# Modulation vectors for later layers: sums down the partitions and a turn through TensorE, or one multiply-and-sum along the row

## The chip, the cores and the metric

The kernel runs on one core of one Trainium2 chip. Its time is the device time of one execution in microseconds (us), the median over several runs. All five engines of the core take part: TensorE (PE; its weight loads are shown as PEld), VectorE (DVE), ScalarE (ACT), GpSimd (POOL) and SyncE (SP), which only issues DMAs.

## The reference

One step of a two-layer network on 128 prompt tokens and 512 latent tokens, model width 2048, all in float32. Each layer has a modulation (adaLN) with a shift, a scale and a gate for each of the two token groups:

```python
def adaln(cvec, w, b):
    mod = jax.nn.silu(cvec) @ w + b          # w: (2048, 3 * 2048)
    return jnp.split(mod, 3, axis=-1)
...
    for l in range(DEPTH):
        sh_p, sc_p, g_p = adaln(c_ctx[None, :], w_ada[l], b_ada[l])
        sh_s, sc_s, g_s = adaln(c, w_ada[l], b_ada[l])
        hp = rmsnorm(xp, norm_pre[l]) * (1.0 + sc_p[:, None]) + sh_p[:, None]
        hs = rmsnorm(xs, norm_pre[l]) * (1.0 + sc_s[:, None]) + sh_s[:, None]
        ...                                  # mixer of the layer: op, os_
        xp = xp + g_p[:, None] * rmsnorm(op, norm_post[l])
        xs = xs + g_s[:, None] * rmsnorm(os_, norm_post[l])
```

Layer 0's mixer has windowed attention (8 heads, "A") and neighbourhood attention (8 heads, "B") side by side; layer 1's is a retention. Both have an input and an output projection, which hold nearly all of the arithmetic.

## The kernel before

Activations lie transposed: features on the 128 partitions (16 tiles of 128), 640 tokens along the row. The projections run in float32 precision out of rounded parts: every weight tile of 128x512 (`wraw`) is split into a rounded part `whi` (ACT, L291) and the rest `wlo` (DVE, L292), every activation into `hi` and `lo`, and PE multiplies hi by whi, lo by whi and hi by wlo (L1370, L1311).

The program is one hand-ordered stream. Its main loop goes over slots; a slot is one split weight tile and 24 to 30 matmuls on it. `ahead(s)` splits the tile of slot s+4 and loads that of slot s+7. Four split tiles fit in SBUF, so a split waits until PE has finished the slot four before. Ahead of each slot `step_all()` moves four lanes one step on, in this order: `chain` (norms after a projection), `rope` (rotation of A's queries and keys), `heads` (attention blocks: scores on PE, softmax on DVE and ACT, transposes, values) and `adal` (the later modulation). A lane takes one new item each step, and the later stages of an item come at the steps after it. Every engine works through its own queue in program order.

The modulation of layer 0's shift and scale is needed at once and is made by PE at the start. The **later modulation**, layer 0's gate and layer 1's shift, scale and gate (8192 outputs for each of two vectors), is spread by the lane `adal` over the slots of layer 0's input projection, which runs from 150 to 990 us. There the weights have their *input* features on the partitions, as 256 tiles of 128x512 (`adaraw`, L787). For each tile and each of the two vectors, DVE multiplies the tile by the vector's value of its partition and adds it to an accumulator `adaacc` of 128x512 (L804). For one tile in five or so, the second vector's share goes another way: ACT scales the tile in place (L801), and POOL adds it (L802). After 16 tiles, a quarter's sums still lie spread over the 128 partitions. They are split into three bfloat16 parts (`adab`, L812, L814, L818), and PE adds them up over the partitions, 128 columns at a time, each as weights against a column of ones:

```python
    def ada_cols(ids, dst, q4):
        if ids[0] == 0:
            parts3["ps"] = dense()
        ps = parts3["ps"][:, 8 * (ids[0] > 0):]
        for c in range(4):
            for v in range(2):
                for i in ids:
                    mm(ps[:, 2 * c + v:2 * c + v + 1], lhsT=parts3[i, v][:, 128 * c:128 * c + 128], rhs=ones16,
                       start=(i == ids[0]), stop=(i == ids[-1]))
```

It is called twice for each of the 16 quarters, first for one part (8 matmuls), then for two (16). DVE copies and adds the results into `gg`, `sh` and `am` (L832, L834), and `ada_fin` adds the bias and makes scale and gate ready. `dense()` is one of five PSUM banks that the projections use in turn.

The prediction also speaks of two places in layer 0's attention. A query of an A head is rotated by `rope_item`: swapped quarters by DMA into `rp`, products on DVE (L574) and POOL (L575), and their sum on DVE (L578). One step after the sum is issued, PE's first score of the head (L722) follows. In a block's softmax DVE adds the bias and takes the maximum in one instruction (L688, `tensor_tensor_reduce`), ACT takes the exponential (L698), DVE normalizes (L705), and PE transposes (L742).

Of the kernel before, what the change touches and what calls it, by code (L numbers as in the profile page):

```python
# [11 lines left out]
F32 = mybir.dt.float32  # L12
F32R = mybir.dt.float32r
BF16 = mybir.dt.bfloat16
AF = mybir.ActivationFunctionType
ALU = mybir.AluOpType
# [3 lines left out]
KT = 16  # L20
# [5 lines left out]
EPS = 1e-6  # L26
SCALE = 128 ** -0.5
NEG = -1e30
ADA_UNITS = (2, 1, 2, 2, 2, 1, 2, 2, 2)
PLACE = {("w_in_even", "W"): 2, ("w_in_even", "X"): 1, ("w_out_even", "W"): 1, ("w_in_odd", "W"): 2,  # L30
         ("w_in_odd", "X"): 1, ("w_out_odd", "W"): 0}
GAPS = (2, 1)
# [130 lines left out]
def body(tc, io):  # L163
    nc = tc.nc
    top = ExitStack()
    top.enter_context(tc.manual_schedule())
    main = top.enter_context(tc.tile_pool(name="main", bufs=1))
# [4 lines left out]
    lo = main.tile([128, KT, T], F32R, name="lo")  # L172
    y = main.tile([128, KT, T], F32, name="y")
    ident = main.tile([128, 128], F32, name="ident")
    ones = main.tile([128, 128], F32, name="ones")
    ones16 = main.tile([128, 1], BF16, name="ones16")
    cols = main.tile([128, 2, 5, KT], F32, name="cols")
    gn = main.tile([128, KT], F32, name="gn")
    sink = main.tile([128, 8], F32, name="sink")
    cvec = main.tile([128, KT, 2], F32, name="cvec")  # L180
    mhalf = main.tile([128, 1], F32, name="mhalf")
    sh = [main.tile([128, KT, 2], F32, name=f"sh{l}") for l in range(2)]
    am = [main.tile([128, KT, 2], F32, name=f"am{l}") for l in range(2)]
    gg = [main.tile([128, KT, 2], F32, name=f"gg{l}") for l in range(2)]

    def bg(tag):
        return psb.tile([128, 512], F32, name="ps_" + tag, tag=tag)

    def dense():
        return psd.tile([128, 512], F32, name="ps_d", tag="d")  # L190

    mm = nc.tensor.matmul
# [3 lines left out]
    nc.sync.dma_start(cvec, io["cT"])  # L196
    nc.sync.dma_start(cols, io["cols"])
    nc.sync.dma_start(ident, io["ident"])
    nc.vector.memset(ones, 1.0)
    nc.vector.memset(mhalf, -0.5)  # L200
    nc.vector.memset(ones16, 1.0)

    def rstd_cols(acc, nt, pool, out, alloc=None):

        ps = alloc() if alloc else bg("T")
        accs = acc if isinstance(acc, list) else [acc]
        for t in range(nt):
            for i, ac in enumerate(accs):
                mm(ps[:, t:t + 1], lhsT=ac[:, 128 * t:128 * t + 128], rhs=ones[:, :1],
                   start=(i == 0), stop=(i == len(accs) - 1))  # L210
        v = pool.tile([128, 5], F32, name="msq")
        nc.vector.tensor_scalar(v[:, :nt], ps[:, :nt], 1.0 / D, EPS, op0=ALU.mult, op1=ALU.add)
        nc.gpsimd.tensor_tensor(out[:, :nt], v[:, :nt], mhalf.to_broadcast([128, nt]), op=ALU.pow)
# [8 lines left out]
    def rstd_bc(dg, nt, out, alloc=None):  # L222
        for b0 in range(0, nt, 4):
            n = min(4, nt - b0)
            ps = alloc() if alloc else bg("S")
            for t in range(n):
                mm(ps[:, 128 * t:128 * t + 128], lhsT=ones, rhs=dg[:, b0 + t, :], start=True, stop=True)
            nc.scalar.activation(out[:, 128 * b0:128 * (b0 + n)], ps[:, :128 * n], AF.Copy)
        return ps

# [39 lines left out]
    for job, (w, kind, role, col, gs) in enumerate(STREAM):  # L270
        u0 = FIRST_UNIT[BLOCK_AT[w, kind, col]]
        n = UNITS[kind]
# [23 lines left out]
    with ExitStack() as st:  # L296
        s1 = st.enter_context(tc.tile_pool(name="s1", bufs=1))
        sraw = st.enter_context(tc.tile_pool(name="sraw", bufs=SRAW))
        x = y
# [66 lines left out]
        def norm_a():  # L366
            rstd_cols(acc[0], 5, s1, rcol, dense)
# [129 lines left out]
    adal = Lane(done)  # L497
# [27 lines left out]
    at = L0.enter_context(tc.tile_pool(name="at", bufs=1))  # L525
# [252 lines left out]
            block(j)  # L778


    ada_raw = {}
    NADA = 16 * KT

    def ada_load(i):
        if i < NADA:
            ada_raw[i] = at.tile([128, 512], F32, name="adaraw", bufs=4)
            nc.sync.dma_start(ada_raw[i], io["ada1"][i])  # L787

    accs = {}

    def ada_unit(i, pool=False):
        kt = i % KT
        r = ada_raw.pop(i)
        if kt == 0:
            for v in range(2):
                accs[v] = at.tile([128, 512], F32, name="adaacc", bufs=2)
                nc.vector.tensor_scalar(accs[v], r, cvec[:, kt, v:v + 1], None, op0=ALU.mult)
        else:
            for v in range(2):
                if v == 1 and pool:  # L800
                    nc.scalar.activation(r, r, AF.Copy, scale=cvec[:, kt, 1:2])  # L801
                    nc.gpsimd.tensor_tensor(accs[1], accs[1], r, op=ALU.add)  # L802
                else:
                    nc.vector.scalar_tensor_tensor(accs[v], r, cvec[:, kt, v:v + 1], accs[v], op0=ALU.mult, op1=ALU.add)  # L804
    parts3 = {}

    def ada_part(i):

        for v in range(2):
            parts3[i, v] = at.tile([128, 512], BF16, name="adab", bufs=4)  # L810
            if i < 2:
                nc.scalar.activation(parts3[i, v], accs[v], AF.Copy)  # L812
            else:
                nc.vector.tensor_tensor(parts3[i, v], accs[v], parts3[1, v], op=ALU.subtract)  # L814

    def ada_less():
        for v in range(2):
            nc.vector.tensor_tensor(accs[v], accs[v], parts3[0, v], op=ALU.subtract)  # L818

    def ada_cols(ids, dst, q4):  # L820

        if ids[0] == 0:
            parts3["ps"] = dense()
        ps = parts3["ps"][:, 8 * (ids[0] > 0):]
        for c in range(4):
            for v in range(2):
                for i in ids:
                    mm(ps[:, 2 * c + v:2 * c + v + 1], lhsT=parts3[i, v][:, 128 * c:128 * c + 128], rhs=ones16,
                       start=(i == ids[0]), stop=(i == ids[-1]))
        d = dst[:, 4 * q4:4 * q4 + 4, :].rearrange("p c v -> p (c v)")  # L830
        if ids[0] == 0:
            nc.vector.tensor_copy(d, ps[:, :8])  # L832
        else:
            nc.vector.tensor_tensor(d, d, ps[:, :8], op=ALU.add)  # L834

    def ada_fin(l, what, dst):
        for v in range(2):
            d = dst[:, :, v]
            nc.vector.tensor_tensor(d, d, cols[:, l, 2 + what, :], op=ALU.add)
            if what == 1:  # L840
                nc.vector.scalar_tensor_tensor(d, d, 1.0, cols[:, l, 0, :], op0=ALU.add, op1=ALU.mult)
            if what == 2:
                nc.vector.tensor_tensor(d, d, cols[:, l, 1, :], op=ALU.mult)

    ada_items = []
    for q, (l, what) in enumerate(((0, 2), (1, 0), (1, 1), (1, 2))):
        dst = {0: sh, 1: am, 2: gg}[what][l]
        for q4 in range(4):
            i0 = KT * (4 * q + q4)
            for n in ADA_UNITS:  # L850
                ada_items.append([[lambda i=i0 + j, p=(j == 1 and i0 % KT < 12): ada_unit(i, p) for j in range(n)],
                                  [lambda i=i0 + 4 + j: ada_load(i) for j in range(n)]])
                i0 += n
            ada_items.append([[lambda: ada_part(0), ada_less]])
            ada_items.append([[lambda: ada_part(1)]])
            ada_items.append([[lambda d=dst, q=q4: ada_cols((0,), d, q), lambda: ada_part(2)], [lambda d=dst, q=q4: ada_cols((1, 2), d, q)]
                              + ([lambda l=l, w=what, d=dst: ada_fin(l, w, d)] if q4 == 3 else [])])
    i = 0
    while i < len(ada_items):
        it = ada_items[i]  # L860
        if len(it) == 2 and i % (len(ADA_UNITS) + 3) == len(ADA_UNITS) + 2 and i + 1 < len(ada_items):
            it = [x + z for x, z in zip(it, ada_items[i + 1])]
            i += 1
        i += 1
        adal.add([lambda st=st: [f() for f in st] for st in it])
    for i in range(4):
        ada_load(i)


# [45 lines left out]
    def queue_chain(l, gi):  # L915
# [11 lines left out]
        def n1(acc):  # L927
            def f():
                st["rc"] = cp.tile([128, 5], F32, name="rcol", bufs=2)
                rstd_cols(c[acc, gi], nt, cp, st["rc"])  # L930
                st["dg"] = rstd_diag(st["rc"], nt, cp)
            return f
# [397 lines left out]
    s = 0  # L1330
    while s < NS:
        job, kind, role, gs, unit, half, i, ni, w = slots[s]
# [13 lines left out]
        i0 = KP // 4 if role[0] == "rest" else 0  # L1346
# [94 lines left out]
def prepare(inp):  # L1441
    f = np.float32
    a = {k: np.asarray(v) for k, v in inp.items()}
    m = constants()
# [26 lines left out]
    wada = a["w_ada"]  # L1471
    w0 = wada[0].reshape(4, 4, 128, 3, 16, 128)
    ada0 = w0[:, :, :, 0:2].transpose(4, 0, 2, 1, 3, 5)
    m["ada0"] = np.ascontiguousarray(ada0.reshape(64, 128, 1024))
    w1 = wada.reshape(2, 16, 128, 12, 512)
    pieces = [(0, i) for i in range(8, 12)] + [(1, i) for i in range(12)]
    m["ada1"] = np.ascontiguousarray(np.stack([w1[l, :, :, p, :] for l, p in pieces], 0).reshape(256, 128, 512))
    W = {n: a[n][0] for n in ("w_in_even", "w_out_even", "w_in_odd", "w_out_odd")}
    wg = W["w_in_even"][:, 4608:]
    m["wfirst"] = np.ascontiguousarray(np.stack(  # L1480
# [32 lines left out]
```

## Time and profile before

| | |
|---|---|
| time, median of 3 runs | 2534.35 us (2533.91 to 2534.43) |
| the profiled execution's own time | 2534.7 us |
| its span in the trace | 2532.9 us |
| busy in the span: PE, DVE, ACT, POOL | 97%, 59%, 40%, 15% |
| matmuls | 17808 |
| mean granted clock of PE | 0.995 |
| HBM traffic | 325.51 MB read, 15.99 MB written |

The trace is of the profiled execution, whose span is 1.8 us shorter than its own time. Busy time of an engine is that in which at least one of its instructions runs; instructions of one engine overlap a little at their ends, so that a group's count times its mean can be above its busy time. "Idle before" is the engine's idle time just before an instruction, put down to what released it.

### The profile page before, as it was taken

How to read it: one execution, taken by the hardware profiler on the slowest of the kernel's cores; microseconds unless marked ns; L12 is line 12 of the kernel's file. 1: busy time of each engine (PE TensorE's matmuls, PEld its weight loads, DVE VectorE, ACT ScalarE, POOL GpSimd, SP SyncE). 2: the span in 40 equal slices, each digit the busy share in tenths (PEclk: the TensorE clock that was granted, in tenths of full speed). 3: DMA queues.
4: the chain of work that ended last, by engine and by line, in shares of the span. 5: the costliest groups of instructions: out<-in, count | busy, mean ns of one | idle time of the engine just before them, and what ended most of it. 6: DMA issues, size and time to landing. Idle time of an engine off the chain costs nothing.

```text
span 2532.9 us, 45640 instructions
## 1 busy us (share of the span) xinstructions
PE 2459.2 (97%) x17808; PEld 2383.1 (94%) x17808; DVE 1499.3 (59%) x2834; ACT 1006.8 (40%) x2140; POOL 389.6 (15%) x445
## 2 busy tenths in 40 slices
PE   5999999999999999999999999999999999999997
PEld 3699898999999999998999999999999999999996
DVE  6578787787777875338853535353525355363364
ACT  3233454443343335445653333233323333344443
POOL 1012221112112110114200101010101011011132
PEclk9999999999999999999999999999999999999998
DMA  9855444445545532436543121212121221215374
GB/s 373 319 171 178 148 138 145 127 136 183 174 155 172 174 132 86 160 131 224 188 159 128 63 80 63 88 59 86 61 88 59 80 80 63 80 59 179 124 238 130
DMA packets 186441, 347.12 MB, mean 137 GB/s; under 512 B 20912, under 2 KB 45872, under 8 KB 185712
## 3 DMA queue, kind: packets, MB, share of 16 engines
q1 hardware_dynamic: 182368, 333.25, 39.7%
q0 software_dynamic: 3712, 10.82, 1.2%
q8 instruction: 139, 2.28, 0.4%
q14 instruction: 78, 0.64, 0.1%
q10 hardware_dynamic: 144, 0.13, 0.0%
HBM read 325.51 MB, written 15.99 MB: 135 GB/s over the span
## 4 chain that ended last, share of the span: by engine, by line
PE 69%; DVE 4%; issue 2%; ACT 1%; DMA 1%; POOL 0%; SPq 0%; DVEq 0%; ACTq 0%; POOLq 0%
PE ps_d L1370 49%; PE ps_d L1311 12%; PE ps_O L1250 2%; DVE wlo L292 1%; DVE adaacc L804 1%; PE ps_O L1154 1%; PE ps_S L1154 1%; PE ps_O L753 1%; PE ps_T L1228 1%; ACT whi L291 1%; PE ps_S L1242 1%; DMA wraw<-i_wpack 0%; PE ps_T L742 0%; DVE y L974 0%; PE ps_T L1141 0%
## 5 line engine op out<-in xcount | busy, mean ns | idle before, releaser
L1370 PE MATMUL ps_d<-hi,whi 128*128 128x384 f32 (+1 forms) x3808 | 999.0, 316 | 0.7 <-ACT whi L291 0.6
L1370 PE MATMUL ps_d<-hi,wlo 128*128 128x384 f32 (+1 forms) x3808 | 977.1, 310 | 7.4 <-DVE wlo L292 7.0
L1370 PE MATMUL ps_d<-lo,whi 128*128 128x384 f32 (+1 forms) x3808 | 972.6, 309 | 0.0
L292 DVE TENSOR_TENSOR wlo<-wraw,whi 128x512 fp32r<-128x512 f32 x732 | 565.2, 775 | 595.8 <-ACT whi L291 591.0
L1370 PEld LDWEIGHTS ps_d<-hi,whi 128*128 128x128 f32 x3808 | 632.8, 189 | 11.7 <-issue 4.3
L1370 PEld LDWEIGHTS ps_d<-hi,wlo 128*128 128x128 f32 x3808 | 628.9, 189 | 13.0 <-DVE wlo L292 12.2
L1370 PEld LDWEIGHTS ps_d<-lo,whi 128*128 128x128 f32 x3808 | 628.2, 188 | 0.0
L291 ACT ACTIVATE whi<-wraw 128x512 fp32r<-128x512 f32 x732 | 454.8, 626 | 432.9 <-PE ps_d L1370 220.6
L804 DVE SCALAR_TENSOR_TENSOR adaacc<-adaraw,cvec,adaacc 128x512 f32<-128x512 f32 x400 | 276.8, 743 | 5.8 <-POOL adaacc L802 5.7
L802 POOL TENSOR_TENSOR adaacc<-adaacc,adaraw 128x512 f32<-128x512 f32 x80 | 103.0, 1288 | 714.0 <-ACT adaraw L801 711.2
L1311 PE MATMUL ps_d<-whi,hi 128*128 128x256 f32 x960 | 150.9, 287 | 0.8 <-ACT qT L654 0.8
L1311 PE MATMUL ps_d<-whi,lo 128*128 128x256 f32 x960 | 144.3, 280 | 0.0
L1311 PE MATMUL ps_d<-wlo,hi 128*128 128x256 f32 x960 | 144.3, 280 | 0.0
L801 ACT ACTIVATE adaraw<-adaraw,cvec 128x512 f32<-128x512 f32 x80 | 57.9, 724 | 207.7 <-DVE adaacc L804 149.3
L1311 PEld LDWEIGHTS ps_d<-whi,hi 128*128 128x128 f32 x960 | 128.0, 188 | 4.9 <-issue 1.4
L1311 PEld LDWEIGHTS ps_d<-wlo,hi 128*128 128x128 f32 x960 | 126.5, 188 | 0.0
L1311 PEld LDWEIGHTS ps_d<-whi,lo 128*128 128x128 f32 x960 | 126.5, 188 | 0.0
L890 POOL TENSOR_TENSOR acc<-acc,sq 128x384 f32<-128x384 f32 (+1 forms) x56 | 56.1, 1002 | 425.9 <-ACT sq L886 425.6
L698 ACT ACTIVATE p<-p,small 128x384 f32<-128x384 f32 (+1 forms) x64 | 42.9, 671 | 148.3 <-DVE small L690 148.3
L1146 DVE SCALAR_TENSOR_TENSOR fr<-ps_T,kdec,fr 128x256 fp32r<-128x256 f32 x64 | 31.0, 484 | 95.8 <-ACT fr L1145 95.8
L1235 ACT ACTIVATE sS<-sT 128x128 fp32r<-128x128 f32 x40 | 12.4, 311 | 147.9 <-DVE sT L1234 147.9
L1262 POOL TENSOR_TENSOR mv<-mv,mhalf 128x1 f32<-128x1 f32 x40 | 22.1, 552 | 299.5 <-DVE mv L1261 299.5
(248 smaller groups left out, 2427.8 us busy)
## 6 DMA issues: line engine op xcount, KB each, us to landing
wraw<-i_wpack SPq DMA_DIRECT2D x732, 256.0 KB, 2.8
adaraw<-i_ada SPq DMA_DIRECT2D x256, 256.0 KB, 2.7
sraw<-i_ada SPq DMA_DIRECT2D x64, 512.0 KB, 6.3
y<-i_xTp SPq DMA_DIRECT2D x4, 1280.0 KB, 8.6
wf<-i_wfirst SPq DMA_DIRECT2D x20, 256.0 KB, 5.9
bias<-i_biasB POOLq DMA_DIRECT2D x8, 640.0 KB, 4.9
x_scratch<-y SPq DMA_DIRECT2D x8, 384.0 KB, 3.8
xres<-x_scratch SPq DMA_DIRECT2D x8, 384.0 KB, 6.9
```

The lines of the kernel that those rows point to most:

```text
L291: nc.scalar.activation(h, r, AF.Copy)
L292: nc.vector.tensor_tensor(l, r, h.bitcast(F32), op=ALU.subtract)
L698: nc.scalar.activation(p[:, :nk], src, AF.Exp, bias=sm[:, 0:1], accum_out=sm[:, 1:2])
L801: nc.scalar.activation(r, r, AF.Copy, scale=cvec[:, kt, 1:2])
L802: nc.gpsimd.tensor_tensor(accs[1], accs[1], r, op=ALU.add)
L804: nc.vector.scalar_tensor_tensor(accs[v], r, cvec[:, kt, v:v + 1], accs[v], op0=ALU.mult, op1=ALU.add)
L890: nc.gpsimd.tensor_tensor(c["acc", gi], c["acc", gi], sq[:, :w], op=ALU.add)
L1146: nc.vector.scalar_tensor_tensor(t[:, 1, :], ps[:, :256], R["kdec"][:, d, h:h + 1], t[:, 0, :].bitcast(F32), op0=ALU.mult, op1=ALU.subtract)
L1154: mm(ps[:, 256 * d:256 * d + 256], lhsT=k[:, kp, 128 * d:128 * d + 128], rhs=v[:, vp, ch, :], start=(i == 0), stop=(i == 2))
L1250: mm(ab, lhsT=t["q"][:, qp, d, :], rhs=t["S"][d][sp].rearrange("p i e -> p (i e)"), start=(d == 0 and i == 0), stop=(d == 1 and i == 2))
L1311: mm(pss[j][:, o:o + 256], lhsT=xp[:, k, c0:c0 + 128], rhs=wp[:, 256 * kk:256 * kk + 256], start=(i == 0 and kk == 0 and p == 0 and t in ( ...
L1370: mm(pss[gi][:, :b - a], lhsT=wp[:, 128 * kk:128 * kk + 128], rhs=xp[:, k, a:b], start=(k == 4 * i0 and p == 0), stop=(k == KT - 1 and p = ...
```

## The change

The weights of the later modulation are laid out with the *output* features on the partitions and the input features along the row: 64 groups of 128 outputs, each in two halves of 1024 inputs, 128 tiles of 128x1024. The two vectors lie along the row as well, the same on all partitions (`adacb`, 1024 inputs of both at a time, 1 MB), and ACT applies SiLU to them there. For a tile and a vector DVE does one `tensor_tensor_reduce`: product with the vector, summed along the row into one column of `gg`, `sh` or `am`; the second half starts from the first half's sum. ACT, POOL and PE do nothing for it any more, apart from SiLU. The 128 units (one tile, both vectors) are spread over 172 steps of the lane. Half-way the other half of the vectors is loaded, with five empty steps behind it. Tiles have two buffers of 4 KB a partition where they had four of 2 KB.

```diff
-ADA_UNITS = (2, 1, 2, 2, 2, 1, 2, 2, 2)
+ADA_SLOTS = 172
+ADA_REST = 5
...
-                mm(ps[:, 128 * t:128 * t + 128], lhsT=ones, rhs=dg[:, b0 + t, :], start=True, stop=True)
+                mm(ps[:, 128 * t:128 * t + 128], lhsT=one.to_broadcast([128, 128]), rhs=dg[:, b0 + t, :], start=True, stop=True)
...
-    NADA = 16 * KT
+    ada_dst = [(gg[0], 0, 2), (sh[1], 1, 0), (am[1], 1, 1), (gg[1], 1, 2)]
+    NADA = 2 * 4 * KT
+    cb = at.tile([128, 2, 1024], F32, name="adacb")
...
-            ada_raw[i] = at.tile([128, 512], F32, name="adaraw", bufs=4)
+            ada_raw[i] = at.tile([128, 1024], F32, name="adaraw", bufs=2)
             nc.sync.dma_start(ada_raw[i], io["ada1"][i])
...
-    def ada_unit(i, pool=False):
-        kt = i % KT
+    def cb_load(half):
+        nc.sync.dma_start(cb, io["cb"][half])
+
+    def cb_silu(v):
+        nc.scalar.activation(cb[:, v, :], cb[:, v, :], AF.Silu)
+
+    def ada_unit(i):
+        half, f = divmod(i, 4 * KT)
+        q, n = divmod(f, KT)
+        dst, l, what = ada_dst[q]
         r = ada_raw.pop(i)
-        if kt == 0:
-            for v in range(2):
-                accs[v] = at.tile([128, 512], F32, name="adaacc", bufs=2)
-                nc.vector.tensor_scalar(accs[v], r, cvec[:, kt, v:v + 1], None, op0=ALU.mult)
-        else:
-            for v in range(2):
-                if v == 1 and pool:
-                    nc.scalar.activation(r, r, AF.Copy, scale=cvec[:, kt, 1:2])
-                    nc.gpsimd.tensor_tensor(accs[1], accs[1], r, op=ALU.add)
-                else:
-                    nc.vector.scalar_tensor_tensor(accs[v], r, cvec[:, kt, v:v + 1], accs[v], op0=ALU.mult, op1=ALU.add)
...
         for v in range(2):
...
+            out = r if v else at.tile([128, 1024], F32, name="adajunk")
+            d = dst[:, n, v:v + 1]
+            nc.vector.tensor_tensor_reduce(out=out, in0=r, in1=cb[:, v, :], scale=1.0, scalar=d if half else 0.0,
+                                           op0=ALU.mult, op1=ALU.add, accum_out=d)
+        if half and n == KT - 1:
+            ada_fin(l, what, dst)
...
+    at_unit = 0
+    for s in range(ADA_SLOTS):
+        if at_unit * ADA_SLOTS <= s * NADA:
+            if at_unit == NADA // 2:
+                adal.add([lambda: cb_load(1), None, lambda: cb_silu(0), lambda: cb_silu(1)])
+                for _ in range(ADA_REST):
+                    adal.add([None])
+            adal.add([lambda i=at_unit: ada_unit(i), lambda i=at_unit: ada_load(i + 2)])
+            at_unit += 1
+        else:
+            adal.add([None])
+    cb_load(0)
+    for v in range(2):
+        cb_silu(v)
+    for i in range(2):
         ada_load(i)
```

The functions `ada_part`, `ada_less` and `ada_cols` go, and the old list of items with them.

The first place is DVE's queue from the rotated query of the first A head to the head's first softmax. Before, one step's share of the modulation is up to four instructions of 512 columns between the rope's product (L574) and its sum (L578):

```order
L574 TENSOR_TENSOR qT<-rp,cosT 128x512
L804 SCALAR_TENSOR_TENSOR adaacc<-adaraw,cvec,adaacc 128x512 x4
L292 TENSOR_TENSOR wlo<-wraw,whi 128x512
L578 TENSOR_TENSOR qT<-qT,rp 128x512
L804 SCALAR_TENSOR_TENSOR adaacc<-adaraw,cvec,adaacc 128x512 x4
```

Of the change, at the same head (line numbers are lower by one here; `ISA` on two tiles is the multiply-and-sum, the `ISA` of 128x1 behind it reads its sum out):

```order
L573 TENSOR_TENSOR qT<-rp,cosT 128x512
L805 ISA adajunk,sh_77<-adaraw,adacb 128x1024
L805 ISA sh_77 128x1
L805 ISA adaraw,sh_77<-adaraw,adacb 128x1024
L805 ISA sh_77 128x1
L291 TENSOR_TENSOR wlo<-wraw,whi 128x512
L577 TENSOR_TENSOR qT<-qT,rp 128x512
```

The four instructions of 512 columns have become one unit of two instructions of 1024; the split and the rope's sum stay behind it.

The second place is ACT's queue during the last A head, where the change reloads the vectors. Before:

```order
L698 ACTIVATE p,small<-p,small 128x384
L700 ACTIVATE small<-sink,small 128x1
L801 ACTIVATE adaraw<-adaraw,cvec 128x512
L744 ACTIVATE pt<-ps_T 128x512
L698 ACTIVATE p,small<-ps_S,small 128x128
L700 ACTIVATE small<-sink,small 128x1
L291 ACTIVATE whi<-wraw 128x512
L744 ACTIVATE pt<-ps_T 128x384
```

Of the change:

```order
L697 ACTIVATE p,small<-p,small 128x384
L699 ACTIVATE small<-sink,small 128x1
L795 ACT_TABLE_LOAD
L795 ACTIVATE adacb<-adacb 128x1024
L743 ACTIVATE pt<-ps_T 128x512
L697 ACT_TABLE_LOAD
L697 ACTIVATE p,small<-ps_S,small 128x128
L699 ACTIVATE small<-sink,small 128x1
L795 ACT_TABLE_LOAD
L795 ACTIVATE adacb<-adacb 128x1024
L290 ACTIVATE whi<-wraw 128x512
L743 ACTIVATE pt<-ps_T 128x384
```

The scaling of a tile is gone from ACT, and two SiLU instructions with three table loads stand between two exponentials; the program has 31 table loads in all where it had 27.

## Rows read from the trace of the kernel before

**Rows 1.** The page's first part: busy us, share of the span, instructions.

```profile
PE 2459.2 (97%) x17808; PEld 2383.1 (94%) x17808; DVE 1499.3 (59%) x2834; ACT 1006.8 (40%) x2140; POOL 389.6 (15%) x445
```

**Rows 2.** All engines' busy us in the stage 150 to 990, then clock, DMA.

```profile
150.00:990.00 840.00, 821.86 (x6087) 799.17 (x6086) 650.24 (x1254) 353.20 (x761) 161.92 (x174) 0.99 0.48 153
```

**Rows 3.** Waits of PE, 150 to 1000 us: total us, times, longest.

```profile
PE ps_S L722 <- DVE qT L578: 11.0, 5, 4.3
PE ps_T L742 <- DVE p L705: 3.8, 5, 1.7
PE ps_S L725 <- DVE small L688: 1.6, 1, 1.6
```

**Rows 4.** Two windows of 40 us: engines' busy us, PEclk, DMA share.

```profile
270.00:310.00 40.00, 39.21 (x278) 37.58 (x276) 29.94 (x66) 18.38 (x41) 8.58 (x9) 0.96 0.40 126
390.00:430.00 40.00, 35.72 (x250) 34.47 (x249) 30.86 (x61) 18.56 (x43) 10.12 (x10) 0.91 0.38 119
```

**Rows 5.** Timeline of weight loads (PEld): start us, duration us, line, count.

```profile
192.15 0.36 PEld L828 LDWEIGHTS <-adab 128*128 128x128 bf16 x8
192.44 0.30 PEld L1370 LDWEIGHTS ps_d<-hi,whi 128*128 128x128 f32 x2
...
195.68 0.30 PEld L1370 LDWEIGHTS ps_d<-hi,wlo 128*128 128x128 f32 x2
196.09 0.47 PEld L828 LDWEIGHTS <-adab 128*128 128x128 bf16 x16
196.48 0.30 PEld L1370 LDWEIGHTS ps_d<-hi,whi 128*128 128x128 f32 x2
```

**Rows 6.** DVE groups by form, 150 to 990: busy us, mean ns, idle before.

```profile
L804 DVE SCALAR_TENSOR_TENSOR adaacc<-adaraw,cvec,adaacc 128x512 f32<-128x512 f32 x400 | 276.8, 743 | 5.8 <-POOL adaacc L802 5.7
L292 DVE TENSOR_TENSOR wlo<-wraw,whi 128x512 fp32r<-128x512 f32 x189 | 179.2, 950 | 143.7 <-ACT whi L291 143.4
L688 DVE CUSTOM_DVE_ANT_0 p<-ps_S,bias,sink 128x512 f32<-128x512 f32 x16 | 11.9, 744 | 0.0
L688 DVE CUSTOM_DVE_ANT_0 p<-ps_S,bias 128x512 f32<-128x512 f32 x16 | 10.9, 684 | 2.7 <-PE ps_S L725 1.6 <-PE ps_S L728 1.1
L688 DVE CUSTOM_DVE_ANT_0 p<-ps_S,bias 128x384 f32<-128x384 f32 x16 | 8.8, 550 | 5.3 <-PE ps_S L725 3.6 <-PE ps_S L728 1.7
L688 DVE DVE_READ_ACCUMULATOR2_ANT small<- 128x1 f32 x64 | 5.2, 81 | 0.0
```

**Rows 7.** Busy us of instructions on tile adaacc, 150 to 990.

```profile
150.00:990.00 840.00, 329.40 (x496) 37.54 (x64) 103.03 (x80) 0.99 0.48 153
```

**Rows 8.** Waits of the whole span, ACT's on DVE: us, times, longest.

```profile
ACT adaraw L801 <- DVE adaacc L804: 149.3, 54, 5.7
```

**Rows 9.** Timeline of DVE around the first query head, 262 to 269 us.

```profile
262.11 1.37 DVE L292 TENSOR_TENSOR wlo<-wraw,whi 128x512 fp32r<-128x512 f32 x1 [1.31 <-ACT whi L291]
263.40 0.94 DVE L595 TENSOR_TENSOR y<-y,ps_d 128x128 f32<-128x128 f32 x3
264.26 0.93 DVE L574 TENSOR_TENSOR qT<-rp,cosT 128x512 f32<-128x512 f32 x1
...
267.76 0.68 DVE L292 TENSOR_TENSOR wlo<-wraw,whi 128x512 fp32r<-128x512 f32 x1
268.37 0.68 DVE L578 TENSOR_TENSOR qT<-qT,rp 128x512 f32<-128x512 f32 x1
```

**Rows 10.** Timeline of PE at the same place; brackets: idle time and releaser.

```profile
269.10 0.70 PE L722 MATMUL ps_S<-kT,qT 128*128 128x256 f32 x2 [3.66 <-DVE qT L578]
```

**Rows 11.** DMA issues: KB each, median us from issue to landing.

```profile
sraw<-i_ada SPq DMA_DIRECT2D x64, 512.0 KB, 6.3
bias<-i_biasB POOLq DMA_DIRECT2D x8, 640.0 KB, 4.9
```

**Rows 12.** Timeline of ACT around a table load; the ACTIVATE is a SiLU.

```profile
335.89 1.28 ACT L520 ACT_TABLE_LOAD   x1
337.19 0.83 ACT L520 ACTIVATE y<-ps_d 128x128 f32<-128x128 f32 x3
```

More of the change, by code (lines that the diff above doesn't have):

```diff
@@ L174, in body @@
     ident = main.tile([128, 128], F32, name="ident")
-    ones = main.tile([128, 128], F32, name="ones")
-    ones16 = main.tile([128, 1], BF16, name="ones16")
+    one = main.tile([128, 1], F32, name="one")
     cols = main.tile([128, 2, 5, KT], F32, name="cols")
@@ L198, in body @@
     nc.sync.dma_start(ident, io["ident"])
-    nc.vector.memset(ones, 1.0)
+    nc.vector.memset(one, 1.0)
     nc.vector.memset(mhalf, -0.5)
-    nc.vector.memset(ones16, 1.0)
     def rstd_cols(acc, nt, pool, out, alloc=None):
@@ L208, in rstd_cols @@
             for i, ac in enumerate(accs):
-                mm(ps[:, t:t + 1], lhsT=ac[:, 128 * t:128 * t + 128], rhs=ones[:, :1],
+                mm(ps[:, t:t + 1], lhsT=ac[:, 128 * t:128 * t + 128], rhs=one,
                    start=(i == 0), stop=(i == len(accs) - 1))
@@ L781, in body @@
     ada_raw = {}
-    NADA = 16 * KT
+    ada_dst = [(gg[0], 0, 2), (sh[1], 1, 0), (am[1], 1, 1), (gg[1], 1, 2)]
+    NADA = 2 * 4 * KT
+    cb = at.tile([128, 2, 1024], F32, name="adacb")
     def ada_load(i):
         if i < NADA:
-            ada_raw[i] = at.tile([128, 512], F32, name="adaraw", bufs=4)
+            ada_raw[i] = at.tile([128, 1024], F32, name="adaraw", bufs=2)
             nc.sync.dma_start(ada_raw[i], io["ada1"][i])
-    accs = {}
-    def ada_unit(i, pool=False):
-        kt = i % KT
-        r = ada_raw.pop(i)
-        if kt == 0:
-            for v in range(2):
-                accs[v] = at.tile([128, 512], F32, name="adaacc", bufs=2)
-                nc.vector.tensor_scalar(accs[v], r, cvec[:, kt, v:v + 1], None, op0=ALU.mult)
-        else:
-            for v in range(2):
-                if v == 1 and pool:
-                    nc.scalar.activation(r, r, AF.Copy, scale=cvec[:, kt, 1:2])
-                    nc.gpsimd.tensor_tensor(accs[1], accs[1], r, op=ALU.add)
-                else:
-                    nc.vector.scalar_tensor_tensor(accs[v], r, cvec[:, kt, v:v + 1], accs[v], op0=ALU.mult, op1=ALU.add)
@@ L805, in body @@
-    parts3 = {}
-    def ada_part(i):
-        for v in range(2):
[L810 to L834, printed above, removed]
+    def cb_load(half):
+        nc.sync.dma_start(cb, io["cb"][half])
@@ L843, in ada_fin @@
                 nc.vector.tensor_tensor(d, d, cols[:, l, 1, :], op=ALU.mult)
[L845 to L866, printed above, removed]
+    at_unit = 0
[13 more added lines that the diff above has]
+    for i in range(2):
         ada_load(i)
@@ L1474, in prepare @@
     m["ada0"] = np.ascontiguousarray(ada0.reshape(64, 128, 1024))
-    w1 = wada.reshape(2, 16, 128, 12, 512)
-    pieces = [(0, i) for i in range(8, 12)] + [(1, i) for i in range(12)]
-    m["ada1"] = np.ascontiguousarray(np.stack([w1[l, :, :, p, :] for l, p in pieces], 0).reshape(256, 128, 512))
+    w1 = np.concatenate([wada[0][:, 4096:], wada[1]], 1).T.reshape(4 * KT, 128, 2, 1024)
+    m["ada1"] = np.ascontiguousarray(w1.transpose(2, 0, 1, 3).reshape(8 * KT, 128, 1024))
+    cc = np.stack([a["c_ctx"].reshape(2, 1024), a["c"][0].reshape(2, 1024)], 1)
+    m["cb"] = np.ascontiguousarray(np.broadcast_to(cc[:, None], (2, 128, 2, 1024)))
     W = {n: a[n][0] for n in ("w_in_even", "w_out_even", "w_in_odd", "w_out_odd")}
```

## The prediction

> **What bounds the kernel now.** I read the page's first part first: PE is busy for 97% of the span [rows 1]. The edit touches one stage, layer 0's input projection, so the next view is the windows of that stage. From 150 to 990 us PE is busy for 821.86 of 840 us, DVE for 650.24 (77%), ACT for 353.20 and POOL for 161.92 [rows 2]. PE is the bound there, and DVE has a quarter of its time free. A change therefore pays only by what it takes out of PE's queue, or out of the waits in which PE stands still; microseconds saved on ACT or POOL count for nothing by themselves.
>
> [...] The waits of PE in the stage: 11.0 us for the rotated queries, 3.8 us for normalized probabilities, 1.6 us for a maximum [rows 3], all three late DVE work. [...] And the weight loads' timeline, for what the 24 column matmuls of a quarter really take of PE's time.
>
> Why is DVE late with a quarter of its time free? The waits of ACT answer: it stood for 149.3 us, 54 times, with its scaling of a tile, since DVE had not yet read that tile for the other vector [rows 8]. Behind the scaling in ACT's queue is the next split `whi`, and DVE's `wlo` waits for that: the row at 262.11 shows 1.31 us of it. The engines wait for each other in a ring. And that `wlo`, beside POOL's addition, takes 1.37 us, where the next one, at 267.76, takes 0.68 [rows 9]; over the stage its mean is 950 ns [rows 6].
>
> **The change part by part.**
>
> *PE's columns go.* In the timeline the 8 loads of the first call start at 192.15 and the next slot's at 192.44: 0.29 us. The second call is seen against the pace: the two loads ahead of it start at 195.68 and take 0.30, so the next slot would have begun at 195.97 and begins at 196.48: 0.51 us, a short wait for `adab` in it [rows 5]. 0.80 us for a quarter, 16 quarters: **12.8 us**. Over all sixteen I allow 11.5 (without the wait) to 15.
>
> *DVE's work changes form.* The instructions on `adaacc`, the splits into bfloat16 included, took 329.40 us [rows 7]. The new one has a close relative in the trace, the softmax's `tensor_tensor_reduce`: 550 ns for 384 columns and 684 for 512 with a constant as start, 1.05 ns a column, so 684 + 512 x 1.05 = 1220 ns for 1024; 744 for 512 with a start from SBUF, so 1280; and 81 ns to read the sum [rows 6]. One of its operands is in PSUM; the nearest row with both in SBUF is L804, 743 ns for 512 [rows 6], which gives the same 1280. A unit is two of them, about 2.65 us, and 128 units 339 us: 10 more than before. Against that `wlo` loses POOL's company: (0.95 - 0.69) x 189 = 49 us. DVE falls to some 611 us, 73%. Nothing of that is on the path as long as DVE is ahead of PE.
>
> *The ring is cut.* ACT no longer touches the tiles, so `whi` follows PE at once. I walk DVE's queue at the first A query, by the rows of the order: product, unit, `wlo`, sum. With three additions before the product the step is 0.94 + 0.93 + 2.65 + 0.68 + 0.68 = 5.9 us by the rows for these instructions [rows 9], and the sum is due two steps after the step's start, 7 us at a slot of 12 x 0.29 = 3.5 us (the pace of the two loads at 195.68 [rows 5]). It comes in time, where before it ended at 269.05 and PE had stood for 3.66 us [rows 9, 10]. At the later heads the order of the change often has no unit at all between product and sum. Of the 11.0 us I keep 1 and take **10.0**. Of the other 5.4 I take half, **2.7**: these are softmax steps, in which the work itself fills most of a slot. For both the bounds are nothing, as new waits might take their place, and all of it.
>
> *The clock.* 0.04 x 40 + 0.09 x 40 = 5.2 us of work lost at the lower level [rows 4]. [...]
>
> *The reload half-way.* SP's queue has the 1 MB load behind unit 63's tile loads; weights are seven slots ahead there, so no tile is late for it. ACT gets two SiLUs and four table loads more. A table load takes 1.28 us, and the SiLUs behind it start 0.02 us after its end; three of them, 640 columns in all, take 0.83 us [rows 12], so 1024 columns at most 1.33. Together 7.8 us of ACT, which is 42% busy over the stage [rows 2], in two steps of about 4.4 us (840 us for 189 splits [rows 2, 6]). ACT is late there by 3 us at most, while the transposed probabilities it copies are due one step on. I charge **2 us**, between 0 and 5, as the load may land late too: 640 KB take 4.9 us [rows 11], so 1 MB at most twice that by estimate, against two steps.
>
> [...]
>
> *Hidden at no cost.* The first 1 MB and its two SiLUs stand in ACT's queue ahead of the split for slot 4, which PE needs four slots, 14 us, after the first; by the same estimate the load takes under 9.8 us and the SiLUs under 2.7. Tiles: the load for unit i+2 waits for unit i to end, and the unit comes two steps later at the earliest. That leaves 2 x 4.4 - 2.65 = 6.2 us, or 4.4 us where no head runs, for 512 KB. By rows that takes from under 4.9 (640 KB, alone) to 6.3 us (512 KB in a full queue) [rows 11]. So DVE may stand up to 2 us now and then; `wlo` has three slots of lead, and one step in four has no unit. The column of ones read with stride 0 serves a few matmuls. The lane takes 178 steps where it took 177 items, so nothing is left over for the end of the stage.
>
> Sum: 12.8 + 10.0 + 2.7 + 4.2 - 2 = 27.7 us. The profiled execution's own 2534.7 is 0.35 above the median, its span lies 1.8 below. 2534.7 - 27.7 = 2507.0, less 0.35 for the median: **2507 us**.
>
> **The rivals.** 0.2% (5 us) is about what a measurement of this kernel can tell from no change.
>
> *Only the columns count.* DVE stays at three quarters, now in blocks of 2.65 us that nothing can pass, and tiles with two buffers; the softmax's waits grow as the rope's shrink. For it: rows 3 are all DVE's lateness, and a step with a unit and a softmax holds about 5 us against a slot of 4.4. Against it: the ring is gone. Then 2534.35 - 12.8 + 2 = 2523.5.
>
> *The gain is eaten.* As before, but 80 attention blocks lose 0.15 us more each behind a block: another 12 us, 2535, no change.
>
> *DVE becomes the bound, slower.* If the new instruction takes two beats a column with both operands in SBUF, it is 0.15 + 1024 x 2.1 ns = 2.3 us, a unit 4.8. DVE's other work is (650.24 - 329.40 - 49) / 189 = 1.44 us a slot, and there are 128/189 = 0.68 units a slot: 4.7 us against PE's (840 - 28)/189 = 4.3. Then 189 x 0.4 = 75 us come on top of 2507: 2582. It decides from a unit of 4.2 us on. L804's 743 ns for two operands in SBUF [rows 6] speak against it.
>
> **How the numbers follow.** Forecast, with its own range of 2498 (15 + 11.0 + 5.4 + 5.2 - 0 saved) to 2518: 0.58. Only the columns, 2518 to 2527: 0.24. Eaten, 2528 to 2540: 0.09. DVE-bound: 0.09. The predicted time is the first one's. 2498 to 2527 holds the first two, 0.82. Faster by over 0.2% is below 2529.3: 0.82; within 0.2%: 0.08; slower: 0.10.
>
> **What would show it.** Right: no matmul of one column in the stage, 384 fewer in all; the new instruction at 1.2 to 1.3 us; `wlo` in the stage near 700 ns; PE's wait for the rotated query below 2 us in all; clock 1.00 in the windows of the stage; the end of the stage some 28 us earlier and everything behind it unchanged. Wrong: PE waiting for `p` or `wlo` by more than 6 us in the stage, DVE waiting for `adaraw` by more than 2 us at a time, or the new instruction above 2 us.

## The result: 39.6 us faster, 3 us beyond the range

The changed kernel takes 2494.77 us (median of 4 runs, 2493.65 to 2495.88), the kernel before 2534.39 beside it: a ratio of 0.9843, with a 95% interval of 0.9831 to 0.9854. The forecast was 2507 and the range ended at 2498. The gain comes out of the one stage, and the rest of the kernel is as before to within 1.4 us. This row is the first use of the gate of layer 0, just behind the stage, in ACT's timeline of the changed kernel (start us, duration us):

```profile
958.43 0.73 ACT L859 ACTIVATE y<-ps_d,gg 128x128 f32<-128x128 f32 x2
```

and this the same instruction in ACT's timeline of the kernel before:

```profile
998.07 0.73 ACT L892 ACTIVATE y<-ps_d,gg 128x128 f32<-128x128 f32 x2
```

It comes 39.6 us earlier, as much as the medians differ by; over their whole spans the two traces differ by 41.0. The page's first part of the changed kernel, to be held against [rows 1], has 384 matmuls fewer and less work on DVE, ACT and POOL:

```profile
PE 2437.9 (98%) x17424; PEld 2368.5 (95%) x17424; DVE 1444.4 (58%) x2817; ACT 936.4 (38%) x2004; POOL 287.6 (12%) x365
```

The windows of the changed kernel's stage, with the columns of [rows 2], and two pieces of 40 us with the times of those in [rows 4]:

```profile
150.00:960.00 810.00, 810.00 (x5756) 794.09 (x5755) 600.99 (x1247) 289.30 (x637) 59.29 (x93) 1.00 0.48 163
...
270.00:310.00 40.00, 40.00 (x281) 38.89 (x280) 33.31 (x78) 18.35 (x45) 5.80 (x9) 1.00 0.49 160
390.00:430.00 40.00, 40.00 (x280) 39.15 (x279) 32.97 (x72) 16.28 (x38) 3.64 (x5) 1.00 0.47 158
```

PE is busy for 810.00 of 810 us, where it lacked 18.1 of 840 before [rows 2], and its granted clock is 1.00 all through. The list of PE's waits from 130 to 1000 us, which held the three rows of [rows 3], is empty.

The costs of the new instructions, from DVE's groups by form, 150 to 960 us (busy us, mean ns, idle before):

```profile
L291 DVE TENSOR_TENSOR wlo<-wraw,whi 128x512 fp32r<-128x512 f32 x194 | 138.3, 715 | 97.1 <-ACT whi L290 92.6 <-DMA adacb<-i_cb 4.2
...
L805 DVE CUSTOM_DVE_ANT_0 adajunk<-adaraw,adacb 128x1024 f32<-128x1024 f32 x64 | 77.9, 1217 | 1.6 <-DMA adaraw<-i_ada 1.6
...
L805 DVE CUSTOM_DVE_ANT_0 adajunk<-adaraw,adacb,gg 128x1024 f32<-128x1024 f32 x32 | 40.9, 1277 | 3.0 <-DMA adaraw<-i_ada 3.0
...
L805 DVE DVE_READ_ACCUMULATOR2_ANT gg<- 128x1 f32 x128 | 10.6, 83 | 0.0
```

The multiply-and-sum takes 1217 ns, and 1277 with the first half's sum as its start, where [rows 6] had given 1220 and 1280. The split `wlo` is down from 950 ns [rows 6] to 715. DVE waited for the new tiles for 6.0 us in all, and PE for none of them. The 4.2 us that the profile puts down to the vectors' load are no cost of it: they lie at the stage's start, ahead of the split at 154.68, and the kernel before has the same 4.18 us there, at 154.84, put down to `whi`.

At the first query head DVE's timeline of the changed kernel answers to [rows 9]:

```profile
256.10 0.95 DVE L594 TENSOR_TENSOR y<-y,ps_d 128x128 f32<-128x128 f32 x3 [2.34 <-PE ps_d L1337]
256.96 0.68 DVE L573 TENSOR_TENSOR qT<-rp,cosT 128x512 f32<-128x512 f32 x1
257.56 1.22 DVE L805 CUSTOM_DVE_ANT_0 adajunk<-adaraw,adacb 128x1024 f32<-128x1024 f32 x1
...
259.98 0.69 DVE L291 TENSOR_TENSOR wlo<-wraw,whi 128x512 fp32r<-128x512 f32 x1
260.58 0.69 DVE L577 TENSOR_TENSOR qT<-qT,rp 128x512 f32<-128x512 f32 x1
```

The rotated query is complete at 261.27. In PE's timeline the score that needs it follows without an idle stretch, where it had stood for 3.66 us [rows 10]:

```profile
263.05 0.59 PE L721 MATMUL ps_S<-kT,qT 128*128 128x256 f32 x2
```

So PE's lost time is gone altogether. What the trace does not say is which part of the edit took it away: the columns, the lighter DVE, ACT's part in the ring, or POOL's additions. Eleven runs, called e1 to e11 further on by the first letters of their labels, tell these apart. Each time stands beside runs of the kernel before on the same chip, whose medians were 2534.0 to 2535.4.

### The profile page after: what moved, and what is told of

It reads as the page before. It is cut to its first block, busy times and chain, and to the rows that moved or that the text cites. A ratio compares the mean times of both kernels' runs of the same rounds, so it can differ in the third digit from the quotient of the medians.

```text
span 2491.9 us, 44269 instructions
## 1 busy us (share of the span) xinstructions
PE 2437.9 (98%) x17424; PEld 2368.5 (95%) x17424; DVE 1444.4 (58%) x2817; ACT 936.4 (38%) x2004; POOL 287.6 (12%) x365
## 4 chain that ended last, share of the span: by engine, by line
PE 95%; DVE 2%; DMA 1%; issue 1%; ACT 0%; POOL 0%; SPq 0%; DVEq 0%; ACTq 0%; POOLq 0%
PE ps_d L1337 65%; PE ps_d L1278 14%; PE ps_d L428 3%; PE ps_O L752 2%; PE ps_O L1217 2%; PE ps_T L741 1%; PE ps_O L1121 1%; PE ps_S L1121 1%; PE ps_S L724 1%; PE ps_T L1195 1%; PE ps_S L341 1%; PE ps_S L727 1%; PE ps_T L341 1%; DVE wlo L291 1%; PE ps_S L1209 1%
## 5 line engine op out<-in xcount | busy, mean ns | idle before, releaser
L291 DVE TENSOR_TENSOR wlo<-wraw,whi 128x512 fp32r<-128x512 f32 x732 | 521.7, 715 | 543.5 <-ACT whi L290 534.7
L743 ACT ACTIVATE pt<-ps_T 128x384 f32<-128x384 f32 (+2 forms) x80 | 39.2, 490 | 124.0 <-PE ps_T L741 122.9
L805 DVE CUSTOM_DVE_ANT_0 adaraw<-adaraw,adacb 128x1024 f32<-128x1024 f32 x64 | 79.4, 1240 | 2.3
L805 DVE CUSTOM_DVE_ANT_0 adajunk<-adaraw,adacb 128x1024 f32<-128x1024 f32 x64 | 77.9, 1217 | 1.6 <-DMA adaraw<-i_ada 1.6
L1221 DVE SCALAR_TENSOR_TENSOR on<-ps_O,qdec,on 128x256 f32<-128x256 f32 x64 | 31.0, 484 | 52.5 <-PE ps_O L1217 50.8
```

Of the source, the lines that this page charges most:

```text
L291: nc.vector.tensor_tensor(l, r, h.bitcast(F32), op=ALU.subtract)
L805: nc.vector.tensor_tensor_reduce(out=out, in0=r, in1=cb[:, v, :], scale=1.0, scalar=d if half else 0.0, op0=ALU.mult, op1=ALU.add, accum_o ...
```

## The experiments

### The columns by themselves

*The kernel before without its 384 column matmuls* (`e1_before_no_columns`). DVE copies from `adab` what it had copied from PSUM, and the sums over the partitions are left out:

```diff
-        if ids[0] == 0:
-            parts3["ps"] = dense()
-        ps = parts3["ps"][:, 8 * (ids[0] > 0):]
-        for c in range(4):
...
-                       start=(i == ids[0]), stop=(i == ids[-1]))
+        ps = parts3[ids[-1], 1]
```

> The kernel before without the 384 column matmuls and their PSUM bank; the copies into gg, sh and am read the parts themselves, so the sums over the partitions are left out. Everything else stays, the ring of DVE, ACT and POOL too. If the columns cost PE what the prediction says, 12.8 us go: 2521.5. If they cost what all 32 calls add up to in the trace (15.9 us from each first load to the next slot's, and some 0.1 us of delay ahead of most), 16 to 18 go: 2517 to 2518. If the waits in the stage hang on the columns as well, PE's waits for the rotated query fall far below 11 us and it comes out below 2510.

Measured: 2528.8 us, ratio 0.9979 [0.9970, 0.9989], only 5.2 us. PE's waits from 150 to 1000 us:

```profile
PE ps_S L722 <- DVE qT L578: 12.1, 5, 4.8
PE ps_T L742 <- DVE p L705: 5.1, 7, 1.8
PE ps_S L725 <- DVE small L688: 1.6, 1, 1.6
PE ps_d L1304 <- ACT qT L654: 1.6, 1, 1.6
```

Each row that answers to one of [rows 3] is as long or longer. The clock in three windows of 40 us went the same way:

```profile
230.00:270.00 40.00, 34.72 (x236) 34.19 (x234) 32.49 (x51) 15.76 (x28) 10.61 (x11) 0.99 0.60 180
270.00:310.00 40.00, 39.15 (x252) 37.93 (x253) 30.41 (x67) 17.34 (x40) 7.51 (x9) 0.93 0.40 127
390.00:430.00 40.00, 35.29 (x226) 34.09 (x225) 30.18 (x61) 19.22 (x43) 10.11 (x10) 0.91 0.39 124
```

DVE was late already, so work taken off PE turned in part into longer waits for DVE: PE's idle time in the stage is 21.9 us, where it was 18.1 [rows 2], and the granted clock of these three windows is 0.99, 0.93 and 0.91, where it was 1.00, 0.96 and 0.91 before.

*The changed kernel with the column matmuls put back* (`e2_after_with_columns`): the same 24 matmuls on constants behind every eight units, with the copies, in the same PSUM banks.

```diff
+        if i % 8 == 6:
+            ada_cols(1)
+        if i % 8 == 7:
+            ada_cols(2)
...
```

> The changed kernel with 8 and 16 column matmuls of bfloat16 put back at the end of every eighth unit (16 times, on constants, with the bank and the two small DVE instructions that take the result away; the output does not change). The same two theories: 12.8 us more, 2507.6, or 16 to 18 more, 2511 to 2513. Either way PE should still wait for no DVE work in the stage; if it does, columns and waits are tied to each other and do not add.

Measured: 2508.07 us, ratio 0.9899 [0.9883, 0.9916]. That is 13.3 us above the changed kernel, and PE has no wait in the stage. Where nothing is late, the columns cost about what the weight loads' timeline [rows 5] said, 12.8 us. The other 26 us of the gain are then left to the waits and the clock.

### The ring of the kernel before, cut in three ways

*ACT scales into a tile of its own* (`e3_before_own_tile`), so that it need not wait for DVE; POOL's 80 additions stay. (They are 80 for 256 tiles, nearly one tile in three, and not one in five or so.)

```diff
-                    nc.scalar.activation(r, r, AF.Copy, scale=cvec[:, kt, 1:2])
-                    nc.gpsimd.tensor_tensor(accs[1], accs[1], r, op=ALU.add)
+                    own = at.tile([128, 512], F32, name="adaown", bufs=1)
+                    nc.scalar.activation(own, r, AF.Copy, scale=cvec[:, kt, 1:2])
+                    nc.gpsimd.tensor_tensor(accs[1], accs[1], own, op=ALU.add)
```

> The kernel before, but ACT writes the scaled share into a tile of its own and POOL adds that, so ACT no longer waits for DVE to have read the tile. POOL's 80 additions stay, and the splits beside them stay slow. Theory ring (the prediction's): DVE was late because ACT's splits stood behind that wait; PE's 18 us of waits and most of the 5 us of clock go, 2512 to 2518. Rival load: DVE was late because it had too much to do, the slow splits above all; the splits' mean stays near 950 ns, more than 12 us of PE's waits stay, 2528 or more.

*All shares on DVE* (`e4_before_all_dve`): neither ACT's scaling nor POOL's additions.

```diff
-                ada_items.append([[lambda i=i0 + j, p=(j == 1 and i0 % KT < 12): ada_unit(i, p) for j in range(n)],
+                ada_items.append([[lambda i=i0 + j, p=False: ada_unit(i, p) for j in range(n)],
```

> The kernel before with all of the multiply-and-adds on DVE: 80 more of 743 ns there, no ACT scaling, no POOL additions. DVE gains 55 us of work and loses about 49 us of slow splits. Ring and load both go with it as far as ACT and POOL cause them: theory ring says 2511 to 2517 with few waits left. If what counts is only how much DVE has to do in a step (three units of two instructions now 3 us in a step), PE's waits stay above 12 us and it comes out at 2528 or more.

*ACT scales in place as before, but POOL adds nothing* (`e11_before_no_pool_add`); the second vector's sums lack those shares, and DVE's wait for POOL's sum, 5.7 us [rows 6], goes too.

```diff
-                    nc.gpsimd.tensor_tensor(accs[1], accs[1], r, op=ALU.add)
```

> The kernel before with ACT's scaling in place, but without POOL's 80 additions (the second vector's sums lack these shares): ring without slow splits. Theory both: most of PE's waits go, 2509 to 2516, against 2508 with the ring cut. Theory spread or ring alone: the ring does it by itself in this order of units, two in most steps, PE's waits stay above 10 us, 2522 or more.

Measured: 2508.04 (ratio 0.9897 [0.9882, 0.9912]), 2507.88 (0.9897 [0.9883, 0.9912]) and 2508.79 us (0.9899 [0.9884, 0.9913]). Each of the three small edits brings the same 26 us. The windows of the stage, first of the kernel with the scaling's own tile:

```profile
150.00:960.00 810.00, 810.00 (x6065) 791.94 (x6066) 657.27 (x1252) 355.96 (x758) 207.87 (x174) 1.00 0.49 159
```

then of the kernel without POOL's additions:

```profile
150.00:960.00 810.00, 808.85 (x6054) 790.17 (x6053) 597.43 (x1249) 353.62 (x755) 58.81 (x94) 1.00 0.50 159
```

In the first DVE does as much as ever, 657.27 us of 810 (81%; before 77% [rows 2]), and `wlo` is slow, 865 ns in the mean, yet PE lacks nothing: it was not DVE's load. In the second ACT waits for DVE with its scaling as before, in its waits over the whole span:

```profile
ACT adaraw L801 <- DVE adaacc L803: 159.0, 70, 6.2
```

That is a little more than the 149.3 us of [rows 8], and DVE waits for `whi` for 156 us. But `wlo` is at 695 ns, and PE's waits in the stage are 0.9 us. So neither the ring alone nor the slow split alone holds PE up in this kernel; both together cost 26 us.

*The scaling's own tile, and no column matmuls* (`e8_own_tile_no_columns`); the sums over the partitions are left out here too. The edit is that of the first of these three and of the first experiment together.

> The kernel before with both: the scaled share in a tile of its own and no column matmuls (the sums over the partitions are left out). Taken by itself the own tile gave 26 us, the columns' removal only 5 us, while put into the changed kernel the columns cost 13. If the columns' removal was eaten by the ring (PE then only waits longer for the late DVE work), it gives its full 13 us here: 2494 to 2496, the changed kernel's time. If 5 us is what the columns are worth and the 13 had another cause, it is 2502 to 2504.

Measured: 2495.01 us, ratio 0.9841 [0.9825, 0.9858]: the time of the changed kernel. Once the ring is cut the columns bring their 13 us, and the two add up to the whole. Nothing is left over for the other parts of the change, the new layout's tiles, buffers and instructions.

### Ring and POOL's additions, given to the changed kernel

*80 POOL additions beside the splits* (`e5_after_pool_adds`), each released by `whi`, so that it lies beside `wlo`:

```diff
+            if 8 <= s < 184 and (s * 80) // 176 != ((s + 1) * 80) // 176:
+                nc.gpsimd.tensor_tensor(pacc["at"].tile([128, 1024], F32, name="adajunk")[:, :512], h.bitcast(F32),
+                                        h.bitcast(F32), op=ALU.add)
...
```

> The changed kernel with 80 POOL additions of 512 columns, each released by the same instruction of ACT as the split on DVE beside it (POOL adds the rounded weights to themselves into the scratch tile; the output does not change). It brings back POOL's company for the splits without the ring. Theory load: splits near 950 ns and more, DVE late, PE's waits in the stage come back, 2505 or more. Theory ring: splits get as slow, but DVE has the time, PE waits for less than 3 us, within 3 us of the changed kernel's 2494.8.

*ACT scales half of the tile in place behind 80 of the 128 units* (`e9_after_ring`), without POOL:

```diff
+        if (i * 80) // NADA != ((i + 1) * 80) // NADA:
+            nc.scalar.activation(r[:, :512], r[:, :512], AF.Copy, scale=cvec[:, 0, 1:2])
```

> The changed kernel with the ring put back: behind 80 of the 128 units ACT scales 512 columns of the tile in place (values that nothing uses; the output does not change), so it waits for DVE's second multiply-and-sum, and the next rounded weights stand behind it. POOL does nothing. Theory ring: ACT waits for DVE some 100 us or more, the splits wait for ACT, PE waits in the stage for rotated queries and probabilities again, 2505 to 2525. If the ring needed POOL's slow splits as well, PE's waits stay under 3 us and it is within 3 us of 2494.8.

*The same, and an addition of POOL on the scaled half* (`e10_after_ring_pool`):

```diff
+            nc.gpsimd.tensor_tensor(at.tile([128, 1024], F32, name="adajunk")[:, :512], r[:, :512], r[:, 512:], op=ALU.add)
```

> The changed kernel with the ring and POOL's company together: the scaling in place behind 80 units, and a POOL addition of 512 columns released by it, beside which the next split runs (into the scratch tile; the output does not change). The ring alone cost 3 us, POOL's additions alone nothing. If the two are needed together (theory both), splits near 950 ns and ACT's waits of 200 us combine: 2502 to 2520. If the changed kernel's even spread of the units, with a step in four free, is what makes it immune (theory spread), it stays below 2500.

Measured: 2494.29 (ratio 0.9843 [0.9828, 0.9858]), 2497.72 (0.9851 [0.9837, 0.9866]) and 2532.28 us (0.9991 [0.9982, 1.0001]). POOL's additions alone cost nothing. The ring alone costs 2 to 3 us, with an interval that overlaps that of the changed kernel. Both together cost 37.5, more than the 26 of the kernel before. In the kernel with the ring alone the ring is there: ACT waits for DVE with its scaling for 198.6 us in the stage, by these three rows,

```profile
ACT adaraw L808 <- DVE gg L805: 105.4, 38, 6.1
ACT adaraw L808 <- DVE sh L805: 50.5, 19, 5.6
ACT adaraw L808 <- DVE am L805: 42.7, 20, 3.5
```

and PE is idle for 1.1 us. The stage's window of the kernel with POOL's additions alone:

```profile
150.00:960.00 810.00, 810.00 (x5756) 793.97 (x5756) 651.27 (x1247) 288.50 (x637) 191.41 (x174) 1.00 0.48 163
```

of the kernel with both:

```profile
150.00:960.00 810.00, 786.13 (x5521) 762.28 (x5520) 633.95 (x1214) 311.04 (x677) 162.80 (x174) 1.00 0.47 159
```

DVE is the busier of the two in the one that loses nothing. With both, 24 us of PE are gone, and its longest waits in the stage are those of the kernel before:

```profile
PE ps_T L741 <- DVE p L704: 15.6, 15, 2.1
PE ps_S L721 <- DVE qT L577: 3.1, 3, 2.5
```

One turn of the ring, from the timeline of DVE, ACT and POOL of the kernel with both:

```profile
171.61 0.08 DVE L805 DVE_READ_ACCUMULATOR2_ANT gg<- 128x1 f32 x1
171.79 0.72 ACT L808 ACTIVATE adaraw<-adaraw,cvec 128x512 f32<-128x512 f32 x1 [3.73 <-DVE gg L805]
172.42 0.61 ACT L290 ACTIVATE whi<-wraw 128x512 fp32r<-128x512 f32 x1
172.60 1.28 POOL L809 TENSOR_TENSOR adajunk<-adaraw 128x512 f32<-128x512 f32 x1 [2.19 <-ACT adaraw L808]
173.07 1.37 DVE L291 TENSOR_TENSOR wlo<-wraw,whi 128x512 fp32r<-128x512 f32 x1 [1.37 <-ACT whi L290]
174.36 1.21 DVE L805 CUSTOM_DVE_ANT_0 adajunk<-adaraw,adacb 128x1024 f32<-128x1024 f32 x1
```

The unit ends, ACT scales, only then splits, and DVE, which has stood idle for 1.37 us, makes the rest of the split beside POOL's addition, in 1.37 us. The scaling releases both, so they fall together: in 76 of the 80 turns that split takes over 1.2 us. From this unit's start at 169.19 to the next one's it is 5.17 us; in the kernel with the ring alone the same turn goes from 170.29 to 174.76, 4.47 us, with `wlo` at 0.69. Over the 80 turns the median from a unit's start to the end of the split is 5.24 us with both and 4.61 with the ring alone. The mean slot of the changed kernel is 4.2 us (810 us for the 194 splits above), so neither turn fits in one, and the slots without a scaling have to make it up. That they can do so for the shorter turn and not for the longer is my reading; that the pair is what costs is measured. What the traces show of the addition is the slow split alone: with both, no engine waits for POOL's addition in the stage, and DVE waits for new tiles for 3.0 us, against 3.4 with the ring alone. Whether any other 0.7 us of DVE in the turn would cost as much, no run here tests.

### How much room DVE had

*A third and a fourth multiply-and-sum in each unit* (`e6_after_three`, `e7_after_four`), on data that lies in SBUF anyway (with `range(2)` in the second):

```diff
+        for _ in range(1):
+            nc.vector.tensor_tensor_reduce(out=at.tile([128, 1024], F32, name="adajunk"), in0=cb[:, 0, :], in1=cb[:, 1, :],
+                                           scale=1.0, scalar=0.0, op0=ALU.mult, op1=ALU.add, accum_out=spare1)
...
```

> The changed kernel with three multiply-and-sums in each unit instead of two (the third on the two vectors, its sum unused; the output does not change). A unit grows from 2.5 to about 3.8 us, 128 times 1.25 is 160 us more of DVE. By the prediction's threshold (4.2 us a unit) PE is still the bound: up to 2500, with waits of a few us at steps with a softmax. If DVE's quarter of free time is used up earlier, since steps with a unit come three in a row, it comes out above 2510.

> The same with four in a unit: about 5 us a unit, above the threshold. By the prediction's formula DVE then sets the stage: (5.0 - 4.2) x 128 = 100 us more, about 2595 to 2610, DVE busy near 100% of the stage. If PE's slack is larger than the formula says, it stays below 2560.

Measured: 2508.48 (ratio 0.9899 [0.9884, 0.9914]) and 2659.0 us (1.0494 [1.0476, 1.0511]), that is 13.7 and 164 us above the changed kernel. The longest waits of PE in the stage with three:

```profile
PE ps_T L741 <- DVE p L704: 4.1, 11, 0.8
PE ps_O L752 <- ACT pt L743: 2.5, 1, 2.5
```

and with four:

```profile
PE ps_T L741 <- DVE p L704: 51.3, 39, 2.3
PE ps_d L1341 <- DVE wlo L291: 23.6, 17, 2.4
PE ps_S L724 <- DVE small L687: 19.8, 9, 3.8
```

The prediction's threshold, a unit of 4.2 us, is no sharp edge. Three multiply-and-sums take 3.6 us (200.67 to 204.31 in DVE's timeline) and cost already, in waits for softmax work: DVE at 730 of 810 us leaves it short at times. Four cost 164 us. Yet 657 us cost nothing, in the kernel with the scaling's own tile, nor did 669 in the one without the columns. So the changed kernel is not bound by DVE and could bear somewhat more of it, but less than one multiply-and-sum a unit.

## Why the prediction was wrong in size and right in kind

**Columns.** Forecast 12.8, measured 13.3 put back, 13.0 taken out where the ring is cut; taken from the kernel before beside each, 13.7 and 14.5. Right, within what these runs can tell.

**The forms and prices of DVE's work.** 1220 and 1280 ns forecast, 1217 and 1277 measured; `wlo` near 700, measured 715; DVE some 611 us over the stage, measured 601. Right. POOL's company as the cause of the slow split is shown by its mean from 150 to 990 us: 853 to 984 ns in e3, e5, e8 and e10, which keep or get the additions, and 693 to 716 in e4, e9 and e11, which have none. In the turn shown above the split begins 0.47 us behind POOL's addition and ends 0.56 us after it, having taken 1.37 us, where it takes 0.69 in the same turn of e9, without the addition. What in the engines makes it slow, no run here shows.

**The ring.** That it was the cause of the waits, and that cutting it frees them, was right. What the prediction did not see is that it needs POOL's addition to do harm: ACT's long waits of [rows 8] alone, which I read as the evidence, cost nothing (e11) or 2 to 3 us (e9).

**The failed step: keeping part of the lost time.** The prediction kept 1 of the 11.0 us of rotated-query waits, half of the 5.4 of softmax, 1 of the 5.2 of clock, and charged 2 for the reload: 14.9 us for these together. The runs give 26 for the same terms (2534 to 2508 in e3, e4 and e11). No run shows the 4.2 us of clock by themselves; what the runs show is a granted clock of 1.00 from 150 to 960 us in the changed kernel, e3, e4 and e11, where two windows of the kernel before had 0.96 and 0.91 [rows 4]. Nothing was left over: the softmax waits went wholly (no wait of PE for `p` is left in e3, e4 or e11), with the same softmax work on DVE, so that they were not "the work itself". That they were the same lateness, handed on along DVE's queue, is how I read it. The reload cost PE nothing. ACT's timeline of the changed kernel shows two of its table loads and the two SiLUs:

```profile
529.06 1.28 ACT L795 ACT_TABLE_LOAD   x1
530.36 1.06 ACT L795 ACTIVATE adacb<-adacb 128x1024 f32<-128x1024 f32 x1
531.32 0.60 ACT L743 ACTIVATE pt<-ps_T 128x512 f32<-128x512 f32 x1
...
533.88 1.28 ACT L795 ACT_TABLE_LOAD   x1
535.17 1.06 ACT L795 ACTIVATE adacb<-adacb 128x1024 f32<-128x1024 f32 x1
```

**The low end of the range.** It was the sum of all upper bounds, 36.6 us, and still 3 short. The bounds were those of the named waits, 16.4 us [rows 3], while the window of the same stage had 840 - 821.86 = 18.1 us without a matmul [rows 2]. With the 5.2 of clock, an estimate from [rows 4], this makes 23.3, against the 26 measured.

**Where the rest of it lies.** Idle time and clock do not make up all that late DVE work costs: 23.3 of 26 us in the kernel before, 24 idle and 3 of clock (two windows at 0.96) out of 37.5 in e10, 8 idle and no clock out of 13.7 in e6. PE's busy time hides a part: in the stage of the kernel before a matmul of 384 columns is on record for 0.34 us in the median, while the next starts 0.18 us after it, so that up to 0.16 us of a stall counts as busy. Counted from each matmul's start to the next one's, the gaps that are over 0.3 us longer than the median of their form hold 26.0 us of such excess in the kernel before and 4.8 in e3. The difference, 21.2, makes with the 5.2 of clock the 26. In the same way e10 has 27.4 us and e6 9.9 us more than the changed kernel; the 4 to 5 us that are still missing between these traces lie in gaps below 0.3 us.

**The rivals.** "Only the columns count" (0.24) fell: no new wait took the place of the old ones. Its mechanism, that gains on PE come back as waits for DVE, is real, but in the kernel before (e1: 13 became 5). "Eaten" and "DVE becomes the bound" fell too; the latter began at a smaller unit than I had worked out, and was steeper.

## What to carry to other kernels

When one engine's wait sits ahead of work for a second, and that second's work releases the first, count the turn of the ring with the durations that its members have when they run together, since the same event releases them (here 1.37 us for the split, not 0.69); a long wait in the ring cost by itself next to nothing here. Take what can be won from the window's idle time and clock over the stage, not from the list of named waits, and know that even this comes out too low (23.3 of 26 us here); and if all those waits go back to one late engine, allow for their going together, not in shares. In the kernel before, one tile of 2 KB a partition for the scaling would have given 26 of the 39.6 us, and so would leaving all shares on DVE.

## What the runs showed of the hardware

Beside a POOL addition of two inputs DVE's split took 1.37 us, where others took 0.68 [rows 9] and 0.69 (e9); over the stage its mean was 950 ns [rows 6], and 695 without the additions (e11). One multiply-and-sum was slow too: the longest in the changed kernel took 2182 ns, the median of its form being 1225; it began at 313.16, beside a product of POOL for the rope that ran from 311.94 for 2.32 us. `scalar_tensor_tensor` was hardly touched before, with 743 ns in the mean [rows 6] against 755 without any addition of POOL (e11); in e3 its mean was 787 ns and its longest took 1.79 us, which I put down to additions that were free to fall beside it there. The two table loads shown above took 1.28 us each, and the next instruction started 0.02 and 0.01 us behind them.
